# A state-space branch: GpSimd in program order, squares behind the exponentials, last gates on VectorE, one transfer per broadcast decay

## The chip, the cores and the metric

The kernel runs on one core of one Trainium2 chip. The metric is the device time of one execution in microseconds (us). The engines are TensorE (PE in the profile; PEld is its weight load), VectorE (DVE), ScalarE (ACT), GpSimd (POOL) and SyncE (SP, which here only issues DMAs).

## The reference, cut to what matters

One layer of a diffusion backbone over 512 latent tokens and 256 context tokens, model width 1024, all in fp32. One input projection feeds an attention branch and a state-space (SSD) branch; both are merged by gates, projected, and followed by a convolutional feed-forward layer. The change lies in the SSD branch alone: 32 heads of 64 channels in 4 groups of 8, a state of 128, chunks of 128 tokens (4 of the latent tokens, 2 of the context), once forward and once backward.

```python
def ssd_scan(xs, la, bm, cm, h0, with_output):
    ...
    cs = jnp.cumsum(ac, axis=-1)
    decay_to_end = jnp.exp(cs[..., -1:] - cs)
    states = jnp.einsum('bcsgn,bgrcs,bcsgrp->bcgrpn', bc, decay_to_end, xc)
    ...
    states = jnp.einsum('bgrzc,bcgrpn->bzgrpn', chunk_decay, states)
    ...
    cb = jnp.einsum('bclgn,bcsgn->bgcls', cc, bc)
    scores = cb[:, :, None] * jnp.exp(segsum(ac))
    y_diag = jnp.einsum('bgrcls,bcsgrp->bclgrp', scores, xc)
    y_off = jnp.einsum('bclgn,bcgrpn,bgrcl->bclgrp', cc, states[:, :-1], jnp.exp(cs))
    return (y_diag + y_off).reshape(Bsz, L, G, R, P).astype(xs.dtype), final

def ssd_output(y, xs, z, d_skip, g):
    y = y + d_skip.reshape(SSD_GROUPS, SSD_HPG, 1).astype(y.dtype) * xs
    return rmsnorm(y.reshape(Bsz, L, D_SSD) * jax.nn.silu(z), g)
```

## The kernel before

**Weights and products.** An fp32 product is computed as three products of rounded parts. A weight tile of 128x1024 is loaded into `wraw` (three buffers; SP issues the load, L177), ScalarE rounds it into `whi` (L183), VectorE takes the rest into `wlo` (L184), each with two buffers, and TensorE uses them in L238, L239 and L241. Weights of the modulation (`wm`) go into the same three `wraw` buffers but are read by VectorE alone, which sums them into `tm` (L811, L813). So the rounding of a weight, the `wm` sums and all else on VectorE stand in one queue.

**Where the branch lies.** The SSD branch runs from about 430 to 728 us of the span, as 4 groups: group 0 to about 500 us, group 1 to 584, group 2 to 664, group 3 to 728. A list of steps, written by hand, weaves a group's steps with the projections of the next group, whose convolution is the `ta` and `tb` steps L1418 to L1429 on ScalarE and VectorE. Small pieces are put between the products of a projection: `gemm` takes one from the list `BETWEEN` at every third of its blocks.

**A group.** `states` sums the context's states (L1606) from weighted inputs `xw` (VectorE, L1575), and steps the backward states from chunk 3 to chunk 1: a product L1587, the old state times a decay on GpSimd (`st`, L1589), and their sum on VectorE (L1590). Then each of the four chunks has two steps:

- `chunk_in` loads the logarithms of the decays, broadcast to all partitions, into `fb` (L1665, 128x8x128 from `cs_d`, one per direction), and the decays for the earlier states into `far` (L1676, from `us_d`, two DMAs of 64 partitions per direction, three buffers). A product gives C times B, whose diagonal VectorE takes as `cbd` (L1686). From it GpSimd makes `coef` (L1690, L1691) and the diagonal blocks `dg` (L1697, two per chunk, not in chunk 0). ScalarE adds to the logarithms (L1707, L1710) and takes the exponential into `E` (L1714); VectorE merges both directions (the mask, L1711) and multiplies by C times B (L1718); GpSimd adds `dg` (L1720).
- `chunk_out` multiplies the states by C (L1738), VectorE weighs these by `far` into `te` (L1740), TensorE forms the chunk's own part from `E` (L1746), GpSimd adds the two `te` into `y` (L1752), and the forward state moves on (L1587 to L1590 again). A piece `late`, put between later products, adds the parts (VectorE, L1761) and multiplies by the gate `zs` (GpSimd, L1763).

At a group's end `gate` stores the 4 gated tiles to `yz_d` (L1774), and `gates_in` loads the next group's gates into `zs` (L1644, two buffers of four tiles). Squares of the gated tiles for the norm follow one group later, on ScalarE into `sq` (L1566, one buffer), and GpSimd sums them into `ssq` (L1567).

**What sets the order.** Each engine carries out its instructions in order. A scheduler chooses that order at build time by readiness in its own model, except that an instruction given to `keep_in_program_order` stays where the program's text has it. SP's DMAs stand in SP's one queue.

Of the kernel before, what the change touches and what calls it, by code (L numbers as in the profile page):

```python
# [9 lines left out]
F32 = mybir.dt.float32  # L10
# [8 lines left out]
P = 128  # L19
# [25 lines left out]
def tile_hybrid_layer(  # L45
# [219 lines left out]
    ao_d = dpool.tile([8, P, L], F32, name="ao_d")  # L265
    yz_d = dpool.tile([16, P, L], F32, name="yz_d")
    cs_d = dpool.tile([64, L], F32, name="cs_d")
    us_d = dpool.tile([64, L], F32, name="us_d")
    dt_d = dpool.tile([64, L + LC], F32, name="dt_d")
    tt_d = dpool.tile([64, 4], F32, name="tt_d")  # L270
    x1_d = dpool.tile([L, D], F32, name="x1_d")
# [156 lines left out]
    with tc.tile_pool(name="spool", bufs=1) as sp:  # L428
# [177 lines left out]
        def square(x_, q, n, k, x):  # L606
            sq = B_[x, k] = tmp(("ta", "tb")[k % 2])[:, :n] if k else q
            S.activation(sq, x_[:, k, :], AF.Square)
# [605 lines left out]
    def tables():  # L1214
# [6 lines left out]
        def rows(a, x):  # L1221
            return 64 * a + 32 * x, 64 * a + 32 * x + 32
# [51 lines left out]
        def far_out():  # L1274
            for a in range(2):
                for x in range(2):
                    (r0, r1), n = rows(a, x), 128 if x else 384
                    nc.sync.dma_start(us_d[32 * a : 32 * a + 32, 384 * x : 384 * x + n], d["U"][r0:r1, :n])

        def to_end():  # L1280
            cs3, la3 = (d[n].rearrange("p (c t) -> p c t", t=P) for n in ("cs", "la"))
# [152 lines left out]
    def h8(a):  # L1434
        return a.rearrange("p (h d) -> p h d", h=8)

    def bc64(a):
        return a.unsqueeze(2).to_broadcast([P, 8, 64])
# [119 lines left out]
    def square(last=False):  # L1558

        yz = SQUARES.pop(0)  # L1560
        if "ssq" not in F:
            F["ssq"] = True
            tc.keep_in_program_order(S.activation(ssq, yz, AF.Square))
        else:
            sq = tmp("ta") if last else zp.tile([P, 512], F32, tag="th", name="sq", bufs=1)
            tc.keep_in_program_order(S.activation(sq, yz, AF.Square))  # L1566
            G.tensor_tensor(ssq, ssq, sq, ALU.add)  # L1567

    def ssd_steps(g):
        d = GR[g]  # L1570
# [13 lines left out]
        def advance(s, dr, c, xw):  # L1584
            z0 = 32 * dr + 8 * g
            ps = misb()
            T.matmul(ps, d["Bk"][:, c, :], xw, start=True, stop=True)  # L1587
            n = new_state(dr)
            G.tensor_tensor(h8(n), h8(s), bc64(eT[:, z0 : z0 + 8, c]), ALU.mult)  # L1589
            V.tensor_tensor(n, n, ps, ALU.add)  # L1590
            return n

# [61 lines left out]

        def chunk_in(c):

            for _ in range(min(c, 1) + c // 3 if g else 0):
                square()
            fb = []
            for dr in range(2):  # L1660
                f = bp.tile([P, 8, P], F32, tag="fb", name="fb", bufs=4)
                a = bass.AP(
                    tensor=cs_d.tensor, offset=cs_d.offset + (32 * dr + 8 * g) * L + c * P, ap=[[0, P], [L, 8], [1, P]]
                )
                nc.sync.dma_start(f, a)  # L1665
                fb.append(f)
            far = []
            for dr in range(2):
                f = bp.tile([P, 4, P], F32, tag="far", name="far", bufs=FAR)
                for u in range(2):  # L1670
                    a = bass.AP(
                        tensor=us_d.tensor,
                        offset=us_d.offset + (32 * dr + 8 * g + u) * L + c * P,
                        ap=[[0, 64], [2 * L, 4], [1, P]],
                    )
                    nc.sync.dma_start(f[64 * u : 64 * u + 64], a)  # L1676
                far.append(f)
            d["far", c] = far
            d["E"] = []

            def products():
                cb = d["cb"] = misb()
                tok = slice(c * P, (c + 1) * P)
                T.matmul(cb[:, :P], d["BT"][:, tok], d["CT"][:, tok], start=True, stop=True)
                cbd = bp.tile([P, 1], F32, tag="cbd", name="cbd", bufs=2)
                V.tensor_tensor_reduce(  # L1686
                    cb[:, P : 2 * P], cb[:, :P], ident, op0=ALU.mult, op1=ALU.add, scale=1.0, scalar=0.0, accum_out=cbd
                )
                coef = d["coef"] = bp.tile([P, 8], F32, tag="coef", name="coef", bufs=2)
                G.tensor_scalar(coef, TT[:, c, 8 * g : 8 * g + 8], cbd, None, ALU.mult)  # L1690
                G.tensor_tensor(coef, coef, bcs[:, 8 * g : 8 * g + 8], ALU.add)  # L1691
                d["dg"] = [diagonal(q) for q in range(2)] if c else None

            def diagonal(q):
                dg = bp.tile([P, 4, P], F32, tag="dg", name="dg", bufs=2)
                w = d["coef"][:, 4 * q : 4 * q + 4].unsqueeze(2).to_broadcast([P, 4, P])
                G.tensor_tensor(dg, ident.unsqueeze(1).to_broadcast([P, 4, P]), w, ALU.mult)  # L1697
                return dg

            def decays():  # L1700
                for q in range(2):
                    E = bp.tile([P, 4, P], F32, tag="E", name="E", bufs=3)
                    eb = misb()
                    F4 = fb[0][:, 4 * q : 4 * q + 4, :]
                    for u in range(4):
                        h = 8 * g + 4 * q + u
                        e0 = S.activation(E[:, u, :], F4[:, u, :], AF.Identity, bias=TX[:, c, 0, h : h + 1])  # L1707
                        if u == 0 and c:
                            tc.keep_in_program_order(e0)
                        S.activation(eb[:, u * P : (u + 1) * P], fb[1][:, 4 * q + u, :], AF.Identity, bias=TX[:, c, 1, h : h + 1])  # L1710
                    V.copy_predicated(E, sel.unsqueeze(1).to_broadcast([P, 4, P]), eb.rearrange("p (h l) -> p h l", h=4))  # L1711
                    d["E"].append(E)
                for E in d["E"]:
                    S.activation(flat(E), flat(E), AF.Exp)  # L1714

            def weighed():
                for q, E in enumerate(d["E"]):
                    V.tensor_tensor(E, E, d["cb"][:, :P].unsqueeze(1).to_broadcast([P, 4, P]), ALU.mult)  # L1718
                    if c:
                        G.tensor_tensor(E, E, d["dg"][q], ALU.add)  # L1720

            if g in BY_BLOCKS and not c:
                decays()
                BETWEEN[1:2] = [lambda f=BETWEEN[1]: (f(), products(), weighed())]
            else:
                products()
                decays()
                weighed()

        def chunk_out(c):  # L1730
            xs, E, far = d["xs"], d["E"], d.pop(("far", c))
            tok = slice(c * P, (c + 1) * P)
            parts = []
            for dr, s in ((0, d["Sf"]), (1, d["Sb"][c])):
                ps = misb()
                for ct in range(4):
                    z = slice(ct * P, (ct + 1) * P)
                    T.matmul(ps[:, z], s[:, z], d["CT"][:, tok], start=True, stop=True)  # L1738
                t = tmp("te")
                V.tensor_tensor(t, ps, flat(far[dr]), ALU.mult)  # L1740
                parts.append(t)

            yd = misb()
            for h in range(8):
                o = yd[64 * (h % 2) : 64 * (h % 2) + 64, (h // 2) * P : (h // 2 + 1) * P]
                T.matmul(o, xs[:, c, h * 64 : (h + 1) * 64], E[h // 4][:, h % 4, :], start=h < 2, stop=c > 0 and h > 5)  # L1746
            dx = None
            if not c:
                dx = bp.tile([P, 512], F32, tag="dx", name="dx", bufs=1)
                G.tensor_tensor(h8(dx), h8(xs[:, c, :]), bc64(d["coef"]), ALU.mult)  # L1750
            y = bp.tile([P, 512], F32, tag="tf", name="y", bufs=1)
            G.tensor_tensor(y, parts[0], parts[1], ALU.add)  # L1752
            if c < 3:
                d["Sf"] = advance(d["Sf"], 0, c, weigh_in(0, c))

            def late():

                for ct in range(0 if c else 4):
                    z = slice(ct * P, (ct + 1) * P)
                    tc.keep_in_program_order(T.matmul(yd[:, z], dx[:, z], ident, start=False, stop=ct == 3, is_transpose=True))  # L1760
                V.tensor_tensor(y, yd, y, ALU.add)  # L1761
                z = d["zt"][:, :, tok]
                G.tensor_tensor(z, y.rearrange("p (a t) -> p a t", a=4), z, ALU.mult)  # L1763

            assert not BETWEEN
            if g < 3:
                BETWEEN.extend([lambda: None] * 4 + [lambda: (late(), turn(1)), turn])
            else:
                BETWEEN.extend([lambda: None] * 2 + [late])
# [650 lines left out]
```

## Time and profile before

| | |
|---|---|
| median of 3 runs | 1233.85 us (1233.82 to 1236.01) |
| the profiled execution, its own time | 1233.18 us |
| its span in the profile | 1231.4 us |
| TensorE busy | 1209.4 us, 98% |
| VectorE, ScalarE, GpSimd busy | 932.3, 682.3, 266.7 us |
| mean granted clock of TensorE | 0.995 |

The profile gives, for each engine, when each instruction began, how long it took and, in brackets, how long the engine had stood idle before it and what released it. The waits are summed per line: "PE mis L1746 <- POOL E L1720: 10.0, 7, 3.7" is 10.0 us in 7 waits, the longest 3.7. A table of stretches gives the busy time of PE, PEld, DVE, ACT and POOL, then the granted clock of TensorE as a fraction, the busy share of the 16 DMA engines, and GB/s. For DMAs a row gives the count, KB each, and the median us from issue to landing. Names are those of the code, without buffer numbers.

### The profile page before, as it was taken

Reading aid. Unit: us, or ns where it says so; the run is one execution under the profiler, and the core shown is the slowest. Engines: PE = TensorE matmul, PEld = TensorE weight load, DVE = VectorE, ACT = ScalarE, POOL = GpSimd, SP = SyncE. Lnnn points to the kernel's source line nnn. Section 1 sums busy time; section 2 is a strip of 40 time slices with the busy share of each in tenths; the row PEclk is TensorE's granted clock in tenths of the full one; section 3 lists DMA queues with packets and bytes.
Section 4 is the critical chain, followed back from the end, with each engine's and each line's share of the span. In section 5 each row is a group of like instructions: output and inputs, shape, how many; then the busy total and the mean of one; then the engine's idle time right before and its main releaser. Section 6 shows DMA issues by size and latency. Waiting matters only on the chain.

```text
span 1231.4 us, 17909 instructions
## 1 busy us (share of the span) xinstructions
PE 1209.4 (98%) x6429; PEld 1009.0 (82%) x6429; DVE 932.3 (76%) x1494; ACT 682.3 (55%) x1267; POOL 266.7 (22%) x278
## 2 busy tenths in 40 slices
PE   9999999999999999999998989999999999999998
PEld 6798888888888888778876868888988888888886
DVE  5857787888565697787885966777688777778787
ACT  5658788787544376465564645223544434436654
POOL 0000121101003555373571752000200110010021
PEclk9999999999999999999999989999999999999999
DMA  9645799744759447347467657677356633436752
GB/s 369 253 136 182 158 248 258 170 153 126 179 168 265 144 131 226 118 134 224 130 167 225 180 185 268 223 252 238 85 126 161 207 112 128 144 96 217 221 185 97
DMA packets 142025, 224.30 MB, mean 182 GB/s; under 512 B 27784, under 2 KB 87344, under 8 KB 141936
## 3 DMA queue, kind: packets, MB, share of 16 engines
q1 hardware_dynamic: 127856, 195.61, 50.8%
q0 software_dynamic: 13792, 27.27, 9.9%
q8 instruction: 51, 0.84, 0.3%
q14 instruction: 38, 0.31, 0.1%
q10 hardware_dynamic: 288, 0.27, 0.1%
HBM read 196.17 MB, written 45.02 MB: 196 GB/s over the span
## 4 chain that ended last, share of the span: by engine, by line
PE 81%; DVE 7%; issue 3%; DMA 3%; POOL 3%; ACT 2%; SPq 0%; DVEq 0%; ACTq 0%; POOLq 0%
PE acc L238 17%; PE acc L239 17%; PE acc L241 17%; PE score L979 3%; PE po L1028 3%; PE pt L1015 2%; PE mis L582 2%; PE mis L2278 2%; PE mis L2276 2%; PE mis L2277 2%; DMA wraw<-wm 1%; PE acc L2278 1%; PE acc L2276 1%; PE acc L2277 1%; PE acc L1098 1%
## 5 line engine op out<-in xcount | busy, mean ns | idle before, releaser
L183 ACT CAST whi<-wraw 128x1024 fp32r<-128x1024 f32 (+1 forms) x115 | 120.1, 1045 | 151.8 <-PE acc L239 109.5
L184 DVE TENSOR_TENSOR wlo<-wraw,whi 128x1024 fp32r<-128x1024 f32 (+1 forms) x115 | 146.6, 1275 | 67.5 <-ACT whi L183 65.2
L238 PE MATMUL acc<-hlh,whi 128*128 128x512 f32 x472 | 195.1, 413 | 0.0
L239 PE MATMUL acc<-hll,whi 128*128 128x512 f32 x472 | 186.2, 395 | 0.0
L241 PE MATMUL acc<-hlh,wlo 128*128 128x512 f32 x472 | 185.9, 394 | 0.0
L238 PE MATMUL acc<-mh,whi 128*128 128x512 f32 x368 | 143.4, 390 | 0.0
L241 PE MATMUL acc<-mh,wlo 128*128 128x512 f32 x368 | 143.4, 390 | 0.0
L239 PE MATMUL acc<-ml,whi 128*128 128x512 f32 x368 | 143.3, 390 | 0.0
L241 PEld LDWEIGHTS acc<-hlh,wlo 128*128 128x128 f32 x472 | 89.4, 189 | 19.6
L238 PEld LDWEIGHTS acc<-hlh,whi 128*128 128x128 f32 x472 | 89.7, 190 | 18.4 <-issue 3.2
L239 PEld LDWEIGHTS acc<-hll,whi 128*128 128x128 f32 x472 | 89.7, 190 | 17.6 <-issue 2.4
L238 PEld LDWEIGHTS acc<-mh,whi 128*128 128x128 f32 x368 | 69.1, 188 | 14.4
L239 PEld LDWEIGHTS acc<-ml,whi 128*128 128x128 f32 x368 | 69.1, 188 | 14.3
L241 PEld LDWEIGHTS acc<-mh,wlo 128*128 128x128 f32 x368 | 69.1, 188 | 14.2
L164 POOL DMA_DIRECT2D dsum<-wdn x24 | 25.2, 1118 | 194.9 <-DVE wlo L1112 184.0
L988 DVE CUSTOM_DVE_ANT_0 p<-score,winm,nsink 128x512 f32<-128x512 f32 (+1 forms) x64 | 51.8, 810 | 15.4 <-PE score L979 13.9
L813 DVE SCALAR_TENSOR_TENSOR tm<-wraw,csil,tm 128x512 f32<-128x512 f32 x56 | 46.3, 827 | 17.1 <-DMA wraw<-wm 16.4
L995 ACT ACTIVATE p<-p,mneg 128x512 f32<-128x512 f32 (+1 forms) x64 | 49.7, 778 | 15.4 <-DVE mneg L988 14.8
L1418 ACT ACTIVATE ta<-acc,half 128x512 f32<-128x512 f32 (+1 forms) x66 | 46.6, 707 | 17.0 <-PE acc L241 15.7
L1023 DVE TENSOR_TENSOR ptl<-pt,pth 128x512 fp32r<-128x512 f32 x72 | 47.5, 685 | 8.8 <-ACT pth L1019 7.7
L238 PE MATMUL acc<-hch,whi 128*128 128x256 f32 x176 | 53.2, 302 | 0.0
L1419 DVE SCALAR_TENSOR_TENSOR ta<-acc,half,ta 128x511 f32<-128x511 f32 (+1 forms) x66 | 43.7, 662 | 12.6 <-ACT ta L1418 12.5
(453 smaller groups left out, 3069.6 us busy)
## 6 DMA issues: line engine op xcount, KB each, us to landing
wraw<-wup SPq DMA_DIRECT2D x44, 512.0 KB, 3.9
dsum<-wdn POOLq DMA_DIRECT2D x24, 704.0 KB, 8.6
wraw<-wm SPq DMA_DIRECT2D x32, 512.0 KB, 4.2
fb<-cs_d SPq DMA_DIRECT2D x32, 512.0 KB, 6.8
wraw<-wx SPq DMA_DIRECT2D x24, 512.0 KB, 4.2
wm<-wm SPq DMA_DIRECT2D x16, 512.0 KB, 8.0
wraw<-wz SPq DMA_DIRECT2D x16, 512.0 KB, 4.1
far<-us_d SPq DMA_DIRECT2D x64, 128.0 KB, 4.0
```

The source lines that it names most:

```text
L183: F["cast"] = S.copy(hi[:, :n], r[:, :n])
L184: F["sub"] = V.tensor_tensor(lo[:, :n], r[:, :n], raw(hi[:, :n]), ALU.subtract)
L238: T.matmul(ps, wh, xh[:, k0 + k, :], start=a, stop=False)
L239: T.matmul(ps, wh, xl[:, k0 + k, :], start=False, stop=False)
L241: T.matmul(ps, wl, xh[:, k0 + k, :], start=False, stop=b)
L813: V.scalar_tensor_tensor(acc, r[:, u * 512 : u * 512 + 512], sc, acc, ALU.mult, ALU.add)
L988: V.tensor_tensor_reduce(p[:, :w], d["ps"][i][:, o0 : o0 + w], m, op0=ALU.add, op1=ALU.min, scale=1.0, scalar=nsink[:, h : h + 1], accum_o ...
L995: S.activation(p, p, AF.Exp, bias=d["mneg"][:, i : i + 1], scale=-1.0, accum_out=d["den"][:, i : i + 1])
L1023: V.tensor_tensor(d["ptl"][x], d["pt"][x], raw(d["pth"][x]), ALU.subtract)
L1418: S.activation(o[:, :n], ps[:, :n], AF.Identity, scale=hcol(base_w, stride + i), bias=hcol(base_b, i))
L1419: x = V.scalar_tensor_tensor(o[:, 1:n], ps[:, 0 : n - 1], hcol(base_w, i), o[:, 1:n], ALU.mult, ALU.add)
L2276: T.matmul(ps, h, wh, start=st, stop=False, skip_group_check=True)
```

## The change

Five things are changed.

1. GpSimd's operations of the branch (`st`, `coef`, `dg`, `E`, `dx`, `y`, the gate, `ssq`) keep the order of the program's text.
2. A square no longer stands at the start of `chunk_in` but behind its exponentials, one each in chunks 1, 2 and 3, and a fourth behind chunk 3's gate.
3. In `chunk_out` the forward state's step stands ahead of `y`.
4. The gate of chunk 3 (four of sixteen) is multiplied on VectorE.
5. `us_d` is laid out anew, so that one DMA of 128 partitions and 256 KB brings what two of 64 partitions and 128 KB brought: 32 loads of `far` for 64. It is written by 8 stores of 128 columns for 4 of up to 384.

```diff
-    us_d = dpool.tile([64, L], F32, name="us_d")
+    us_d = dpool.tile([4, 2, 2, 4, 4, P], F32, name="us_d")
...
         def far_out():
             for a in range(2):
                 for x in range(2):
-                    (r0, r1), n = rows(a, x), 128 if x else 384
-                    nc.sync.dma_start(us_d[32 * a : 32 * a + 32, 384 * x : 384 * x + n], d["U"][r0:r1, :n])
+                    r0, r1 = rows(a, x)
+                    for c in range(1 if x else 3):
+                        o = us_d[3 * x + c, :, a].rearrange("u g j t -> (g j) u t")
+                        nc.sync.dma_start(o, d["U"][r0:r1, c * P : c * P + P])
...
             tc.keep_in_program_order(S.activation(sq, yz, AF.Square))
-            G.tensor_tensor(ssq, ssq, sq, ALU.add)
+            tc.keep_in_program_order(G.tensor_tensor(ssq, ssq, sq, ALU.add))
+
+    def gp(*a):
+        return tc.keep_in_program_order(G.tensor_tensor(*a))
+
+    def gs(*a):
+        return tc.keep_in_program_order(G.tensor_scalar(*a))
...
-            G.tensor_tensor(h8(n), h8(s), bc64(eT[:, z0 : z0 + 8, c]), ALU.mult)
+            gp(h8(n), h8(s), bc64(eT[:, z0 : z0 + 8, c]), ALU.mult)
...
         def chunk_in(c):
 
-            for _ in range(min(c, 1) + c // 3 if g else 0):
-                square()
...
-                for u in range(2):
-                    a = bass.AP(
-                        tensor=us_d.tensor,
-                        offset=us_d.offset + (32 * dr + 8 * g + u) * L + c * P,
-                        ap=[[0, 64], [2 * L, 4], [1, P]],
-                    )
-                    nc.sync.dma_start(f[64 * u : 64 * u + 64], a)
+                a = bass.AP(
+                    tensor=us_d.tensor,
+                    offset=us_d[c, 0, dr, g].offset,
+                    ap=[[32 * P, 2], [0, 64], [1, 512]],
+                )
+                nc.sync.dma_start(flat(f), a)
...
                     if c:
-                        G.tensor_tensor(E, E, d["dg"][q], ALU.add)
+                        gp(E, E, d["dg"][q], ALU.add)
...
                 products()
                 decays()
                 weighed()
+            if g and c:
+                square()
...
-                G.tensor_tensor(h8(dx), h8(xs[:, c, :]), bc64(d["coef"]), ALU.mult)
-            y = bp.tile([P, 512], F32, tag="tf", name="y", bufs=1)
-            G.tensor_tensor(y, parts[0], parts[1], ALU.add)
+                gp(h8(dx), h8(xs[:, c, :]), bc64(d["coef"]), ALU.mult)
             if c < 3:
                 d["Sf"] = advance(d["Sf"], 0, c, weigh_in(0, c))
+            y = bp.tile([P, 512], F32, tag="tf", name="y", bufs=1)
+            gp(y, parts[0], parts[1], ALU.add)
...
-                G.tensor_tensor(z, y.rearrange("p (a t) -> p a t", a=4), z, ALU.mult)
+                x = y.rearrange("p (a t) -> p a t", a=4)
+                if c == 3:
+                    V.tensor_tensor(z, x, z, ALU.mult)
+                else:
+                    gp(z, x, z, ALU.mult)
+                if g and c == 3:
+                    square()
```

GpSimd's row around chunk 2 of group 1, before the change: from the sum `y` of chunk 1 to `y` of chunk 2 (each row is a line of the code, the operation, what it writes and reads, and its shape).

```order
L1752 TENSOR_TENSOR y<-te 128x512
L1567 TENSOR_TENSOR ssq<-ssq,sq 128x512
L1589 TENSOR_TENSOR st<-st,eT 128x512
L1690 TENSOR_SCALAR coef<-TT,cbd 128x8
L1691 TENSOR_TENSOR coef<-coef,bcs 128x8
L1697 TENSOR_TENSOR dg<-ident,coef 128x512 x2
L1763 TENSOR_TENSOR zs<-y,zs 128x4x128
L1567 TENSOR_TENSOR ssq<-ssq,sq 128x512
L1720 TENSOR_TENSOR E<-E,dg 128x512 x2
L1567 TENSOR_TENSOR ssq<-ssq,sq 128x512
L1752 TENSOR_TENSOR y<-te 128x512
```

The same stretch of GpSimd's row after the change; lines 1569, 1572 and 1575 are those of `ssq` and of the two helpers.

```order
L1572 TENSOR_TENSOR st<-st,eT 128x512
L1572 TENSOR_TENSOR y<-te 128x512
L1575 TENSOR_SCALAR coef<-TT,cbd 128x8
L1572 TENSOR_TENSOR coef<-coef,bcs 128x8
L1572 TENSOR_TENSOR dg<-ident,coef 128x512 x2
L1572 TENSOR_TENSOR E<-E,dg 128x512 x2
L1569 TENSOR_TENSOR ssq<-ssq,sq 128x512
L1572 TENSOR_TENSOR zs<-y,zs 128x4x128
L1572 TENSOR_TENSOR st<-st,eT 128x512
L1572 TENSOR_TENSOR y<-te 128x512
```

`E` now stands directly behind `dg`; `ssq` and the gate `zs` have moved behind `E`. The `st` of the third row before is the forward state's step to the end of chunk 2; after the change that is the `st` of the last but one row, behind `E`, `ssq` and `zs` (the `st` of the first row is chunk 1's).

SP's queue from chunk 2 of group 2 to the end of that group, before the change (an `x4` is four DMAs in a row):

```order
L1676 DMA far<-us_d 64x4x128 x4
L177 DMA wraw<-wm 128x1024
L1644 DMA zs<-zs_d 128x512 x4
L1665 DMA fb<-cs_d 128x8x128
L177 DMA wraw<-wg 128x1024
L1665 DMA fb<-cs_d 128x8x128
L177 DMA wraw<-wg 128x1024
L1676 DMA far<-us_d 64x4x128 x4
L1774 DMA yz_d<-zs 128x512 x4
L1665 DMA fb<-cs_d 128x8x128
L1816 DMA ta<-yz_d 128x512 x2
L177 DMA wraw<-wm 128x1024
```

The same stretch after the change:

```order
L177 DMA wraw<-wm 128x1024
L1681 DMA far<-us_d 128x1x512 x2
L1671 DMA fb<-cs_d 128x8x128 x2
L177 DMA wraw<-wg 128x1024 x2
L1681 DMA far<-us_d 128x1x512
L1652 DMA zs<-zs_d 128x512 x3
L1787 DMA yz_d<-zs 128x512 x4
L1652 DMA zs<-zs_d 128x512
L1681 DMA far<-us_d 128x1x512
L1671 DMA fb<-cs_d 128x8x128
L1829 DMA ta<-yz_d 128x512
L177 DMA wraw<-wm 128x1024
```

`wm` has moved ahead of a chunk's `far`; the four `zs` loads have moved behind the next group's first `far`, three ahead of the `yz_d` stores and one behind them; each four `far` are two, now of 128 partitions.

More of the change, by code (lines that the diff above doesn't have):

```diff
@@ L1689, in products @@
                 coef = d["coef"] = bp.tile([P, 8], F32, tag="coef", name="coef", bufs=2)
-                G.tensor_scalar(coef, TT[:, c, 8 * g : 8 * g + 8], cbd, None, ALU.mult)
-                G.tensor_tensor(coef, coef, bcs[:, 8 * g : 8 * g + 8], ALU.add)
+                gs(coef, TT[:, c, 8 * g : 8 * g + 8], cbd, None, ALU.mult)
+                gp(coef, coef, bcs[:, 8 * g : 8 * g + 8], ALU.add)
                 d["dg"] = [diagonal(q) for q in range(2)] if c else None
@@ L1696, in diagonal @@
                 w = d["coef"][:, 4 * q : 4 * q + 4].unsqueeze(2).to_broadcast([P, 4, P])
-                G.tensor_tensor(dg, ident.unsqueeze(1).to_broadcast([P, 4, P]), w, ALU.mult)
+                gp(dg, ident.unsqueeze(1).to_broadcast([P, 4, P]), w, ALU.mult)
                 return dg
```

## The prediction

> **What bounds the kernel now.** I read the page first, then the waits of the tensor engine, then the time line of each engine around the longest of them.
>
> ```profile
> span 1231.4 us, 17909 instructions
> PE 1209.4 (98%) x6429; PEld 1009.0 (82%) x6429; DVE 932.3 (76%) x1494; ACT 682.3 (55%) x1267; POOL 266.7 (22%) x278
> ...
> PE mis L1746 <- POOL E L1720: 10.0, 7, 3.7
> PE mis L1606 <- DVE xw L1575: 3.2, 1, 3.2
> ```
>
> TensorE is the bound: 98% busy, 22.0 us not. Of these, 10.0 us are one wait: the products L1746 stand for `E`, whose last step is GpSimd's sum L1720. Another 3.2 us is a wait for `xw`. Here are these waits in TensorE's time line (start, length, wait in brackets), then VectorE and SP around the second kind:
>
> ```profile
> 544.66 1.95 PE L1738 MATMUL mis<-CT,st 128*128 128x128 f32 x16
> 549.61 1.09 PE L1746 MATMUL mis<-E,xs 128*64 128x128 f32 x16 [2.99 <-POOL E L1720]
> ...
> 631.12 0.66 PE L1746 MATMUL mis<-E,xs 128*64 128x128 f32 x8 [1.00 <-POOL E L1720]
> 632.35 0.66 PE L1746 MATMUL mis<-E,xs 128*64 128x128 f32 x8 [0.58 <-POOL E L1720]
> ...
> 646.99 0.66 PE L1746 MATMUL mis<-E,xs 128*64 128x128 f32 x8 [1.02 <-POOL E L1720]
> ...
> 724.33 0.81 PE L1746 MATMUL mis<-E,xs 128*64 128x128 f32 x8 [3.72 <-POOL E L1720]
> 725.55 1.12 PE L1746 MATMUL mis<-E,xs 128*64 128x128 f32 x8 [0.41 <-POOL E L1720]
> ...
> 660.53 0.48 SPq L177 DMA_DIRECT2D wraw<-wm  x1
> 668.11 1.54 DVE L813 SCALAR_TENSOR_TENSOR tm<-wraw,csil,tm 128x512 f32<-128x512 f32 x2 [5.10 <-DMA wraw<-wm]
> ```
>
> So four places wait for `E`: group 1 chunk 2, group 2 chunks 2 and 3, group 3 chunk 3. After the first and last the clock drops as well (columns: PE, PEld, DVE, ACT, POOL busy, then PEclk, DMA share, GB/s):
>
> ```profile
> 540.00:560.00 20.00, 16.95 (x107) 14.16 (x106) 15.39 (x28) 15.13 (x40) 15.11 (x17) 0.91 0.48 126
> 720.00:740.00 20.00, 15.86 (x71) 12.44 (x70) 12.36 (x16) 9.35 (x15) 8.53 (x6) 0.83 0.55 184
> ```
>
> 0.09 x 20 = 1.8 us and 0.17 x 20 = 3.4 us go there. All that the change could win is then 10.0 + 1.8 + 3.4 + 3.2 = 18.4 us.
>
> **The new order on GpSimd and ScalarE.** Chunk 2 of group 1, GpSimd's rows and VectorE's two that feed them:
>
> ```profile
> 540.96 1.06 POOL L1589 TENSOR_TENSOR st<-st,eT 128x512 f32<-128x512 f32 x1 [0.95 <-DVE st L1590]
> 541.02 0.13 DVE L1686 DVE_READ_ACCUMULATOR2_ANT cbd<- 128x1 f32 x1
> 542.00 0.30 POOL L1690 TENSOR_SCALAR coef<-TT,cbd 128x8 f32<-128x8 f32 x1
> 542.67 2.04 POOL L1697 TENSOR_TENSOR dg<-ident,coef 128x512 f32<-128x512 f32 x2
> 544.67 1.27 POOL L1763 TENSOR_TENSOR zs<-y,zs 128x512 f32<-128x512 f32 x1
> 545.90 1.26 POOL L1567 TENSOR_TENSOR ssq<-ssq,sq 128x512 f32<-128x512 f32 x1
> 547.12 2.49 POOL L1720 TENSOR_TENSOR E<-E,dg 128x512 f32<-128x512 f32 x2
> ...
> 544.09 0.69 DVE L1718 TENSOR_TENSOR E<-E,mis 128x512 f32<-128x512 f32 x1 [0.35 <-ACT E L1714]
> ```
>
> VectorE's `E` was done at 544.78 and `dg` at 544.71, but the sum began at 547.12: `zs` and `ssq`, 2.5 us, stood ahead of it. Now both stand behind. TensorE is ready at 544.66 + 1.95 = 546.6; the sum would run from 544.8 to 547.3, or earlier, since the state's step `st` (1.06 us) no longer stands ahead of `coef`, which then waits only for `cbd` (541.15). ScalarE gains too, since a square no longer stands between the exponentials:
>
> ```profile
> ACT sq L1566 <- POOL ssq L1567: 10.4, 3, 5.5
> ```
>
> These 10.4 us, in which ScalarE stood for a buffer that GpSimd's `ssq` sum held, go; there is one square per chunk, and its predecessor's sum is long done. I take stalls one to three as gone: 2.99 + 1.8 + 1.58 + 1.3 (1.02, and 0.3 that the 10.0 us hold beyond the rows above) = 7.7 us. In group 3 chunk 3 VectorE itself is late:
>
> ```profile
> 720.22 1.30 DVE L1718 TENSOR_TENSOR E<-E,mis 128x512 f32<-128x512 f32 x2
> 720.80 1.27 POOL L1763 TENSOR_TENSOR zs<-y,zs 128x512 f32<-128x512 f32 x1
> 722.02 3.48 POOL L1720 TENSOR_TENSOR E<-E,dg 128x512 f32<-128x512 f32 x2
> ```
>
> Only `zs` (1.2 us) can be passed; 720.9 is then the start, and TensorE was ready at 720.5. I take 1.4 us here and leave the clock's 3.4 as unknown. The order is worth 9.1 us, say 9; its ends are 18.4 (everything goes) and 4 (only the 2.5 us of `zs` and `ssq` in the first stall, and 1.5 us in the three later places together).
>
> What could be late next: `st` stands behind `E`, `ssq` and `zs` now, and VectorE's sum L1590 waits for it. GpSimd needs 1.3 + 1.3 + 1.1 = 3.7 us for the three after `E`; L1590 comes behind 1.1 us of L1746, behind the product L1587, and on VectorE behind two `te`, a `tc` and often a `wlo`. I cost it at nothing, and at up to 2 us a chunk if that cover fails, which the range of the order's gain takes in.
>
> **The last gates on VectorE.** Four times one tensor product, by the nearest row 0.68 us on VectorE, against 1.27 us on GpSimd above:
>
> ```profile
> L1740 DVE TENSOR_TENSOR te<-mis,far x32: 673/676/683, 442.3 to 723.7; 128x512 f32<-128x512 f32 x32
> ```
>
> VectorE is 76% busy, and behind the gate stand the `ta` steps that drain accumulators. 4 x 0.68 = 2.7 us, taken at nothing, since the store behind it starts as much earlier; ends 0 and 2.7.
>
> **The gate loads on SP.** A group's four `zs` loads stood early in the group; three now stand behind its first `far`, and the fourth behind the `yz` stores. A group's last square is later now, and its buffer is what they wait for. They move 1 MB into the stretch where `yz`, `fb` and `wm` queue. Against it, `wm` goes ahead of `far` in chunk 3 of groups 1 and 2. Nothing for both, ends -2 and +3 us.
>
> **One transfer per decay.**
>
> ```profile
> 535.37 2.57 SPq L1676 DMA_DIRECT2D far<-us_d  x4
> ...
> 352.39 1.70 SPq L1278 DMA_DIRECT2D us_d<-dU  x4
> ```
>
> Of 64 `far` loads 32 stay, with twice the bytes each: 32 issues of 0.6 us less on SP, which waits for buffers anyway: nothing. Four more `us_d` stores of 0.4 us, with a weight load behind them: nothing, at most 2 us. What matters is how such a load is spread. Before, its source has 64 equal rows outermost and its target 64 partitions. Now the source is written as 2 blocks, each repeated 64 times. No row of before has a transfer with so few entries outermost, so the trace does not show on how many of the 16 DMA engines it runs. One end: all 16; it is then cheaper than now. The other end: the spread follows the outermost step, and a transfer runs on 2 engines. I take two, because an even cut along the outermost step is what the 64 rows of before allowed and the 2 blocks do not.
>
> The Trainium skill, page "DMA: Bandwidth & Descriptors", section "Rules for kernel authors", says that an outermost dimension smaller than 16 confines a DMA to as many engines at most, and names a leading broadcast; by it this is two engines, and the sum is the one below. No run shows it yet.
>
> The price on two engines:
>
> ```profile
> wraw<-wm SPq DMA_DIRECT2D x32, 512.0 KB, 4.2
> fb<-cs_d SPq DMA_DIRECT2D x32, 512.0 KB, 6.8
> ...
> far<-us_d SPq DMA_DIRECT2D x64, 128.0 KB, 4.0
> ...
> 0.00:60.00 60.00, 58.14 (x391) 42.68 (x392) 40.67 (x89) 32.93 (x62) 2.51 (x11) 1.00 0.81 310
> ...
> 500.00:584.00 84.00, 80.54 (x483) 66.10 (x482) 66.68 (x99) 50.39 (x118) 42.58 (x38) 0.98 0.56 156
> 584.00:664.00 80.00, 77.15 (x475) 64.11 (x474) 65.21 (x95) 50.03 (x118) 44.69 (x39) 1.00 0.59 165
> 664.00:728.00 64.00, 56.69 (x308) 43.76 (x307) 47.35 (x67) 34.86 (x83) 42.46 (x39) 0.97 0.59 186
> ```
>
> A busy DMA engine moved 310 / (0.81 x 16) = 23.9 GB/s in the stretch of large rows. Half of 2 x 128 KB is 131 KB, 5.5 us on each of the two; a group's eight loads are 44 us. Those two also carry a sixteenth of the rest. In group 1 that is 0.56 x 84 = 47 us less the `far` of now (2.1 of 13.1 MB, 7.5 us), 39.5; with 44 it is 83.5 of 84 us: full. Group 2: 47.2 - 7.5 + 44 = 83.7 of 80, 4 us too much. Group 3: 37.8 - 6.7 + 44 = 75 of 64, 11 too much. That makes 15 us from the amount alone, which is the lower end. On top comes the queue: what is issued behind one or two `far` ends 5.5 or 11 us later. `wm` is what hurts, since VectorE takes it in order, with `wlo` and `xw` behind (the 5.1 us wait above, and TensorE's 3.2 us behind that). In front of each of groups 1 to 3 one `wm` stands so; one `far` each makes 16.5 us, two make 33. I take 15 + 16 = 31, ends 15 and 48.
>
> **The sum.** 1231.4 - 9 + 31 = 1253.4 us of span. The profiled execution took 1233.18, 1.8 over its span, so 1255.2; the median of the runs, 1233.85, lies 0.7 above that execution: 1256.
>
> **Rivals.**
> 1. All 16 engines carry the new load; the order's gain stands alone. For it: every transfer of before runs so, as far as landing times tell (4.0 us for `far`, 64 partitions). Against: none of them has a small outermost step. 1233.85 less 9, and some 3 more, as the decays need fewer pieces and `xw`'s wait shrinks: 1222, between 1215 and 1230. This one is faster, and decides as soon as a `far` lands in about 5 us, as before, with 256 KB.
> 2. Two engines, but the rest hides it. For it: weights and `far` are loaded well ahead, here by 10.9 us (issue, then the cast that reads it) and by 18 (the `far` of 535.37 above, then `te`). Against: `wm`, which is not.
>
> ```profile
> 564.19 0.33 SPq L177 DMA_DIRECT2D wraw<-wx  x1
> 575.08 1.04 ACT L183 CAST whi<-wraw 128x1024 fp32r<-128x1024 f32 x1
> ...
> 553.69 0.68 DVE L1740 TENSOR_TENSOR te<-mis,far 128x512 f32<-128x512 f32 x1
> ```
>
> Then only the amount costs, its lower end of 15, against a gain of 9 to 18: 1231 to 1240, say 1235, no change that could be told.
> 3. The order doesn't do what it says: `E` stays late since VectorE's masks are, as in group 3. Against: 544.78 against 547.12 above. It only takes 5 us off the gain, and is in the ranges.
>
> **How the numbers follow.** Two engines and slower 0.56 (1240 to 1280, likeliest 1256); rival 2 0.10; rival 1 0.34. 2.5 us, 0.2%, is about what can be told from no change. Faster: 0.33 of rival 1 and 0.01 of rival 2, 0.34. Same: 0.01 of rival 1 and 0.06 of rival 2, 0.07. Slower: the rest, 0.59. The range must reach over both signs: from 1220 (two thirds of rival 1) to 1277 (most of the likeliest) it holds 0.8.
>
> **What the profile will show.** Right on the order: no L1746 wait for GpSimd in groups 1 and 2, GpSimd's `E` directly behind `dg`, no `sq` wait for `ssq`. Right on the load: `far` lands in 8 us or more, `wraw` and `fb` in well over their 4.2 and 6.8 us, and new waits of VectorE for `wm` and of ScalarE for `fb`, with TensorE behind them, most in group 3. Wrong: `far` lands in 4 to 6 us; then rival 1 holds. It would also be wrong, the other way, if the two engines fall so far behind that whole chunks wait for `far` itself, over 1280.

## The result, and the profile after

| | before | changed |
|---|---|---|
| median | 1234.59 us (1233.82 to 1236.01, 4 runs) | 1267.14 us (1266.48 to 1268.07, 4 runs) |
| ratio to before | | 1.0263, interval 1.0245 to 1.0281 |
| span of the profiled execution | 1231.4 us | 1265.3 us |
| mean granted clock | 0.995 | 0.983 |

The change is slower by 32.5 us. The forecast was slower, 1256 us, with a range of 1220 to 1277.

The page of the changed kernel, its span and TensorE's row:

```profile
span 1265.3 us, 17888 instructions
PE 1219.7 (96%) x6429; PEld 1014.3 (80%) x6429; DVE 933.3 (74%) x1498; ACT 681.6 (54%) x1267; POOL 259.5 (21%) x274
```

The span grew by 33.9 us. TensorE stood for 45.6 us where it had stood for 22.0, which is 23.6; and the same 6429 products took 1219.7 us for 1209.4, 10.3 us more, at a granted clock of 0.983 for 0.995. The waits, summed per line (us in total, times, longest):

```profile
DVE tm L813 <- DMA wraw<-wm: 48.7, 12, 12.9
ACT E L1712 <- DMA fb<-cs_d: 28.1, 6, 13.7
...
PE mis L1614 <- DVE xw L1583: 9.2, 1, 9.2
PE mis L1595 <- DVE xw L1583: 6.5, 2, 4.9
PE acc L238 <- DVE ta L1424: 6.3, 1, 6.3
PE mis L1753 <- POOL E L1572: 5.6, 8, 1.2
```

VectorE waits for `wm` three times as long as before (16.4 us there), ScalarE for `fb`, for which it hardly waited (3.3 us), and TensorE behind both: `wm` and `fb` take 3% each of the chain that ended last. The old wait for `E` (now L1753) is 5.6 us for 10.0, and none is over 1.2; ScalarE's wait of `sq` for `ssq` is 3.1 us, one wait, for 10.4.

What the new loads do shows where little else moves. This is a stretch in which two `far` are on their way, issued from 450.67 on, with no other load of SP behind them until 455.89 (columns: length, then busy time and count of PE, PEld, DVE, ACT, POOL; then PEclk, DMA share, GB/s):

```profile
453.50:455.80 2.30, 2.30 (x11) 1.88 (x10) 1.72 (x3) 2.30 (x10) 2.12 (x3) 1.00 0.13 52
```

0.13 of 16 engines is two engines, and they move 52 GB/s, 26 each. A load of 256 KB is then 5.0 us on them; the prediction had 5.5.

Now the first place where TensorE stands, ahead of group 0: SP's queue, then the chain of waits from there on (start, length, what).

```profile
370.46 3.66 SPq L1681 DMA_DIRECT2D far<-us_d  x2
374.17 7.64 SPq L1652 DMA_DIRECT2D zs<-zs_d  x4
381.86 0.55 SPq L1671 DMA_DIRECT2D fb<-cs_d  x1
382.51 7.15 SPq L177 DMA_DIRECT2D wraw<-wm  x1
```

```profile
382.51 13.28 DMA wraw<-wm
395.81 0.75 DVE tm L813
396.56 0.60 DVE CT L1431
397.17 0.66 DVE tm L813
397.83 0.67 DVE ta L1421
398.52 0.76 DVE ta L1424
399.42 0.55 PE acc L238
```

Two `far`, four `zs` and an `fb` stand ahead of `wm`. SP needs 7.15 us to issue this one `wm`, and it has landed after 13.3. VectorE takes it in order, with the convolution's `ta` behind, and TensorE starts its next product at 399.42 after 6.35 us of waiting.

### The profile page after: what moved, and what is told of

It reads as the page before. It is cut to its first block, busy times and chain, and to the rows that moved or that the text cites. A ratio compares the mean times of both kernels' runs of the same rounds, so it can differ in the third digit from the quotient of the medians.

```text
span 1265.3 us, 17888 instructions
## 1 busy us (share of the span) xinstructions
PE 1219.7 (96%) x6429; PEld 1014.3 (80%) x6429; DVE 933.3 (74%) x1498; ACT 681.6 (54%) x1267; POOL 259.5 (21%) x274
## 4 chain that ended last, share of the span: by engine, by line
PE 75%; DMA 9%; DVE 8%; ACT 4%; issue 3%; POOL 1%; SPq 0%; DVEq 0%; ACTq 0%; POOLq 0%
PE acc L238 15%; PE acc L239 15%; PE acc L241 15%; DMA wraw<-wm 3%; DMA fb<-cs_d 3%; PE score L979 3%; PE po L1028 3%; PE pt L1015 2%; PE mis L582 2%; PE mis L2291 2%; PE mis L2290 2%; PE mis L2289 2%; PE acc L2291 1%; PE acc L2290 1%; PE acc L2289 1%
## 5 line engine op out<-in xcount | busy, mean ns | idle before, releaser
L813 DVE SCALAR_TENSOR_TENSOR tm<-wraw,csil,tm 128x512 f32<-128x512 f32 x56 | 43.7, 780 | 49.5 <-DMA wraw<-wm 48.7
L1712 ACT ACTIVATE E<-fb,TX 128x128 f32<-128x128 f32 x128 | 45.0, 389 | 31.2 <-DMA fb<-cs_d 28.1
L1430 ACT ACTIVATE tb<-ta 128x512 f32<-128x512 f32 (+1 forms) x44 | 23.4, 532 | 56.9 <-DVE ta L1424 56.8
```

The source lines that it names most:

```text
L813: V.scalar_tensor_tensor(acc, r[:, u * 512 : u * 512 + 512], sc, acc, ALU.mult, ALU.add)
```

## The experiments

All twelve were timed against the kernel before on the same chip; the ratio is what is compared.

**On how many engines the load runs.** Five runs change only the form of the `far` loads. With four blocks the order of the branch on SP, VectorE, ScalarE and GpSimd is that of the changed kernel; in the other four some rows of the queues moved along with it.

*Two halves*: the new layout of `us_d`, but two loads per tile.

```diff
+                for u in range(2):
-                    ap=[[32 * P, 2], [0, 64], [1, 512]],
+                    ap=[[0, 64], [1, 512]],
-                nc.sync.dma_start(flat(f), a)
+                nc.sync.dma_start(flat(f)[64 * u : 64 * u + 64], a)
```

> The changed kernel, but each far tile comes by two loads of 64 partitions again (64 equal rows of 2 KB outermost in the source, new layout of us_d kept). Spread theory (the load runs on as many DMA engines as its outermost step has entries, and that is the whole loss): 1222 us, between 1215 and 1230; wraw<-wm lands in about 4 us, and no wait of VectorE for wm over 5 us. Order theory (the new order or the later gate loads lose the time, the load is harmless): 1262 to 1270, as the changed kernel. Layout theory (the 2 KB rows of the new layout are slow to read however they are spread): over 1245.

*Four, eight and sixteen blocks*: `us_d` holds each block 2, 4 or 8 times (a store with a repeated source), and one load per tile reads 4, 8 or 16 blocks.

```diff
-    us_d = dpool.tile([4, 2, 2, 4, 4, P], F32, name="us_d")
+    us_d = dpool.tile([4, 2, 2, 2, 4, 4, P], F32, name="us_d")
...
-                    ap=[[32 * P, 2], [0, 64], [1, 512]],
+                    ap=[[32 * P, 4], [0, 32], [1, 512]],
```

> The changed kernel, but us_d holds each block twice, so that the source of a far load is written as 4 blocks, each repeated 32 times; bytes, rows and number of loads as in the changed kernel, and the order on all engines too. Spread theory: four engines, a load takes 2.8 us on each instead of 5.5, a group's eight 22 us on top of some 40 of 84: no engine is overfull, two far delay what is behind them by 5.5 instead of 11 us: 1235 us, between 1226 and 1245. Theories that blame the order, or the size of 256 KB in one transfer: 1262 to 1270.

> As the run with four blocks, but 8 blocks, each repeated 16 times. Spread theory: eight engines, 1.4 us on each per load: 1224 us, between 1218 and 1232. Order or size theory: 1262 to 1270.

> The changed kernel with us_d holding each block 8 times, so that a far load's source is 16 blocks, each repeated 8 times: one transfer of 128 partitions still. Spread theory: as the run with two halves, 1227 us, between 1224 and 1231. If one transfer for two saves anything of its own: 1221 to 1224. If what the run with eight blocks had left over (6 us above two halves) is the size of the transfer or the copies, not the spread: 1231 to 1234.

*One of two*: the forward `far` as changed, the backward one in two halves.

> The changed kernel, but only the forward direction's far comes in one load of two blocks; the backward one comes in two halves. Two engines then carry 22 us per group beside some 40 of 84 and are not overfull, but a load still takes 5.5 us on each. If the loss is the amount (an overfull pair of engines falls behind): 1230 to 1238 us. If each such load costs the same, whatever the amount: half the way, 1244 to 1250.

The loss below is the ratio less that of two halves, times 1234.6; by the intervals it is good to about 3 us. The third column is an estimate of what a group's eight `far` put on the busiest engine, by the 23.9 GB/s of the prediction.

| run | median | us on the busiest engine, per group | ratio to before | loss |
|---|---|---|---|---|
| changed, 2 blocks | 1267.14 | 44 | 1.0263 (1.0245 to 1.0281) | 39.6 |
| four blocks | 1236.04 | 22 | 1.0017 (1.0003 to 1.0031) | 9.3 |
| one of two | 1234.60 | 25 | 1.0003 (0.9988 to 1.0018) | 7.5 |
| eight blocks | 1232.88 | 11 | 0.9987 (0.9973 to 1.0000) | 5.6 |
| sixteen blocks | 1227.37 | 5.5 | 0.9940 (0.9927 to 0.9954) | -0.2 |
| two halves | 1227.05 | 5.5 | 0.9942 (0.9920 to 0.9964) | 0 |

With 16 blocks the very same transfer of 256 KB costs nothing, and with fewer the loss rises with what stands on the busiest engine: 22 and 25 us cost the same, within the intervals, whether four engines carry all loads or two carry half of them, and 44 us cost four to five times as much. So it is neither the size of the transfer, nor the layout, nor the order. One transfer for two also saves nothing by itself. Two expectations were narrowly missed: eight blocks lie above their 1218 to 1232, and with two halves VectorE's longest wait for `wm` was 5.6 us, not under 5 (5.1 before). With four and eight blocks SP still stood for up to 5.0 and 4.8 us over one `wm`, with sixteen for 0.4.

The spread itself shows where two `far` of the same chunk are under way, with four blocks and with eight (columns as above):

```profile
447.00:449.00 2.00, 2.00 (x10) 1.68 (x9) 1.24 (x2) 2.00 (x8) 1.84 (x3) 1.00 0.26 102
```

```profile
447.40:448.40 1.00, 1.00 (x6) 0.83 (x5) 1.00 (x2) 1.00 (x5) 0.87 (x2) 1.00 0.52 201
```

That is four engines of 16 and eight, at 25 GB/s each. By the rule of the Trainium skill, page "DMA: Bandwidth & Descriptors", section "Rules for kernel authors", an outermost dimension smaller than 16 confines a DMA to as many engines at most; the traces agree (0.13, 0.26 and 0.52 of 16 with two, four and eight blocks), and so does the loss by the load on the busiest engine.

*The load alone*, put into the kernel before:

> The kernel before with the one-transfer loads alone (new layout, stores and loads; order, squares and gates as before). Spread theory: slower by what the changed kernel lost plus the order's gain, 1234.6 + 32.5 + 9 = 1276 us, between 1268 and 1285. Order theory: 1230 to 1236. If the changed kernel's later gate loads or earlier wm are part of the loss, in between: 1245 to 1265.

Measured 1274.70 us, ratio 1.0330 (1.0303 to 1.0358), 40.7 us slower; the same two waits are there:

```profile
DVE tm L813 <- DMA wraw<-wm: 48.0, 14, 13.2
ACT E L1708 <- DMA fb<-cs_d: 24.0, 3, 14.0
```

So the load costs 40 us with the old order and with the new.

*The loads from ScalarE's queue*: `nc.scalar.dma_start` for `nc.sync.dma_start`, nothing else.

> The changed kernel, but the far loads (two blocks outermost, as changed) are issued from ScalarE's queue, so that SP never stands in front of a full queue. If the loss is mostly that SP stands still and nothing behind it starts on any engine: 1228 to 1245 us, unless ScalarE stands in its turn. If it is mostly that two engines have too much to move and every other transfer ends with its share on them: 1250 to 1270.

Measured 1287.45 us, ratio 1.0437 (1.0417 to 1.0456): slower still, above both expectations. The lengths of one DMA issue (ns, least/median/most) of `fb` before, of `fb` in the changed kernel, and of `far` in this run, then ScalarE and SP in this run:

```profile
L1665 SPq DMA_DIRECT2D fb<-cs_d x32: 360/441/969, 363.5 to 690.7; - x32
```

```profile
L1671 SPq DMA_DIRECT2D fb<-cs_d x32: 370/591/6245, 362.7 to 722.2; - x32
```

```profile
L1681 ACTq DMA_DIRECT2D far<-us_d x32: 489/490/7673, 365.7 to 770.2; - x32
```

```profile
366.81 8.21 ACTq L1681 DMA_DIRECT2D far<-us_d  x2
375.07 2.16 ACT L1712 ACTIVATE E<-fb,TX 128x128 f32<-128x128 f32 x7 [8.15 <-issue]
```

```profile
370.27 15.75 SPq L1652 DMA_DIRECT2D zs<-zs_d  x4
```

An issue of `fb` that took at most 1.0 us before takes up to 6.2 in the changed kernel, and in this run a `far` holds ScalarE for up to 7.7 us. Behind it stands whatever else that engine has to do: ScalarE stood 8.15 us ahead of its activation at 375.07. SP did not become free by this: its four `zs`, issued while ScalarE issued the two `far`, took 15.75 us, for 7.64 in the changed kernel. So the run does not divide the loss between this standing and the overfull engines, since SP stood on and ScalarE stood too; that division stays open.

**What the order is worth.** *All of the change but the loads*:

> All of the change but the loads: program order on GpSimd, squares behind the exponentials, the state ahead of y, last gates on VectorE; far and us_d as in the kernel before. If the order is worth what the prediction said and the layout of two 64-partition loads is neutral: as the run with two halves, 1227 us, between 1224 and 1230. If a part of that run's gain came from the new layout (2 KB rows): 1229 to 1233.

*Program order on GpSimd alone*, and *the squares' place alone*:

> The kernel before with program order for GpSimd's operations alone (squares, y, gates and loads as before). If the gain comes from E standing directly behind dg: 1226 to 1229 us, and ScalarE's wait of sq for ssq stays. If the squares' place is what matters (the wait of ScalarE for the sq buffer, 10.4 us before): 1232 to 1236.

> The kernel before with the squares behind the exponentials alone. If the squares' place is what matters: 1226 to 1229 us. If program order is: 1231 to 1236, with waits of L1746 for E that stay at 5 us or more.

*The order, but the last gates on GpSimd*:

> As the run of the order alone, but chunk 3's gates stay on GpSimd. The prediction put the move at nothing: 1226 us, within 1.5 of the order alone. If the 2 us by which the whole order beats the sum of its two tried parts (2.5 and 3.8 of 8.2) come from these gates: 1228.

| run | median | ratio to before |
|---|---|---|
| order alone | 1226.08 | 0.9931 (0.9918 to 0.9943) |
| program order alone | 1231.69 | 0.9977 (0.9966 to 0.9987) |
| squares alone | 1230.46 | 0.9964 (0.9952 to 0.9976) |
| order, gates on GpSimd | 1226.88 | 0.9937 (0.9924 to 0.9949) |

The order is worth 8.2 us by the medians, and the layout nothing that can be told. Each of the two parts measured between its two expectations, so neither alone is the one that matters: program order brought 2.5 us and left ScalarE's wait of `sq` for `ssq` (8.3 us) and 8.0 us of TensorE's waits for `E`, the squares brought 3.8 us and left 6.2 us of waits for `E`. Together they leave 1.5 us, so in these waits the two do more than their sum. In the medians the whole gains 1.8 us more than the two, which the intervals do not tell from nothing; `st` ahead of `y` was not tried apart. The gates make no difference that can be told. Here is chunk 2 of group 1 in the run of the order alone, GpSimd and then TensorE, as shown of before in the prediction, and that run's waits of TensorE:

```profile
539.84 2.04 POOL L1570 TENSOR_TENSOR dg<-ident,coef 128x512 f32<-128x512 f32 x2
541.84 2.54 POOL L1570 TENSOR_TENSOR E<-E,dg 128x512 f32<-128x512 f32 x2
544.34 1.27 POOL L1567 TENSOR_TENSOR ssq<-ssq,sq 128x512 f32<-128x512 f32 x1
545.57 1.28 POOL L1570 TENSOR_TENSOR zs<-y,zs 128x512 f32<-128x512 f32 x1
...
546.20 1.09 PE L1752 MATMUL mis<-E,xs 128*64 128x128 f32 x16
```

```profile
PE mis L1612 <- DVE xw L1581: 3.3, 1, 3.3
PE mis L1449 <- DVE tc L1429: 2.7, 4, 1.0
PE mis L1752 <- POOL E L1570: 1.5, 3, 1.0
```

`E` follows `dg` at once and is done at 544.4, where it had been done at 549.6; TensorE takes it at 546.2 without a wait, where it had waited 2.99 us.

**A version that beats both.** The largest wait left, `xw`, stands behind a `wm` that SP issues behind `yz`, `zs` and `fb`. *wm ahead* is the order alone, with one step of the written list moved in group 3:

```diff
-        prog += s[0:1] + f + b[0:1] + s[1:2] + s[10:11] + m[0:1] + b[1:2]
+        prog += s[0:1] + f + b[0:1] + s[1:2] + (b[1:2] + s[10:11] + m[0:1] if g == 3 else s[10:11] + m[0:1] + b[1:2])
```

> As the run of the order alone, but in group 3 the second weight of the modulation and its sum stand one step later in the list, behind the next projection's first weight, so that SP issues it ahead of fb and yz. If TensorE's wait for xw behind it (3.3 us in the order alone) goes: 1223 us, between 1221 and 1225. If another wait takes its place: 1226 or more.

Measured 1222.12 us, ratio 0.9899 (0.9884 to 0.9915). The wait for `xw` fell to 1.2 us:

```profile
PE mis L1612 <- DVE xw L1581: 1.2, 1, 1.2
```

That is 2.1 us of the 3.7 by which the span is shorter (1220.6 for 1224.3). The rest is in TensorE's products, which took 1205.6 us for 1207.2.

## Why the prediction was right, and where it was off

**The order: 9 us forecast, 8.2 measured.** The stalls went as its rows said, and `E` of chunk 2 was done earlier still than the 547.3 of its working, since VectorE's `E` came earlier too (done at 542.8 for 544.8). VectorE's `te` of group 1's last chunk began 4.4 us earlier than before, against the 4.8 us (2.99 and 1.8) of the first stall. That the sums agree is partly luck: TensorE's waits for `E` fell by 8.5 us (10.0 to 1.5) where the prediction counted 7.3, since in group 3 it gave back 1.4 of 4.1 us and only 1.0 was left; against that, VectorE's `tc` became late (2.7 us in 4 waits, 0.4 before), and not the `st` that it had named.

**Gates at nothing**: 0.9931 and 0.9937, the same. The `zs` loads and `wm`, taken at nothing, were measured only as part of the order alone, which agrees with it.

**Two engines**: right, and so was the sign.

**The load's price: 31 us forecast, 40 measured.** This is the term that was mis-sized, and its division was wrong as well. It had two parts: 15 us because groups 2 and 3 would carry more than the two engines can in their length, and 16 us for one `wm` in front of each of groups 1 to 3. The first `te` of each group in the changed kernel, and below it in the run of two halves:

```profile
449.97 0.68 DVE L1747 TENSOR_TENSOR te<-mis,far 128x512 f32<-128x512 f32 x1
...
536.64 0.68 DVE L1747 TENSOR_TENSOR te<-mis,far 128x512 f32<-128x512 f32 x1
...
625.80 0.68 DVE L1747 TENSOR_TENSOR te<-mis,far 128x512 f32<-128x512 f32 x1
...
716.42 1.27 DVE L1747 TENSOR_TENSOR te<-mis,far 128x512 f32<-128x512 f32 x2
```

```profile
441.77 0.68 DVE L1748 TENSOR_TENSOR te<-mis,far 128x512 f32<-128x512 f32 x1
...
519.58 0.68 DVE L1748 TENSOR_TENSOR te<-mis,far 128x512 f32<-128x512 f32 x1
...
600.31 0.68 DVE L1748 TENSOR_TENSOR te<-mis,far 128x512 f32<-128x512 f32 x1
...
684.89 1.28 DVE L1748 TENSOR_TENSOR te<-mis,far 128x512 f32<-128x512 f32 x2
```

The lag is 8.2, 17.1, 25.5 and 31.5 us, so it grows by 8.2, 8.9, 8.4 and 6.0 per group and by some 8 more to the end. In groups 0 to 2 it does not grow from the first chunk to the third; it comes ahead of group 0 and at the ends of groups, where `far`, `zs`, `fb` and `wm` stand together. In group 3 it grows by 8.5 us between the second chunk and the third, where SP issued a weight `wg` behind two `far` and ScalarE waited for it:

```profile
748.42 1.05 ACT L183 CAST whi<-wraw 128x1024 fp32r<-128x1024 f32 x1 [10.93 <-DMA wraw<-wg]
```

So the sum over a group's length said little: the price is paid in bursts, where a load that is needed soon stands behind `far`. In the prediction's own terms, the places in front of groups 1 to 3, put at 16 us, cost 23 (8.9, 8.4 and 6.0); the place ahead of group 0, which it left out, cost 8; and against the 15 us from the amount, 4 in group 2 and 11 in group 3, stand only the last 8, all in group 3. So two terms were too small, by 7 and by 8, and one too large by 7, and the 9 us by which the price was missed are what is left of that. The prediction saw the mechanism, `wm` behind `far`, but took weights as loaded well ahead and did not see that SP itself would stand. "Most in group 3" was wrong too: the longest waits for `wm` and for `fb`, 12.9 and 13.7 us, stand ahead of group 0.

**The signs in the profile.** The waits of VectorE for `wm` and of ScalarE for `fb`, with TensorE behind them, came as named. The page of the changed kernel gives no landing times for SP's loads, so "8 us or more" is not shown; the chain gives 13.3 us for one `wm`. The waits for `E` in groups 1 and 2 went where the load is harmless (0.5 us left there in the order alone, and 1.0 in group 3), and not fully beside it (5.6 in all). ScalarE's wait of `sq` for `ssq`, which was to go, kept 3.1 us, at the last square of group 3.

**The rivals.** "All 16 engines" is what the runs of sixteen blocks and of two halves show: 1227, inside the 1215 to 1230 given for it. "Hidden by the rest" was wrong for two engines (39.6 us), and nearly right for four (9.3, against a gain of 8). The third, `E` late behind VectorE's masks, is refuted by the order alone, where `E` was early.

## What to carry to other kernels

Before two transfers are merged into one, look at what stands outermost in both its patterns: a broadcast written as "2 blocks, each repeated 64 times" ran on two DMA engines at 52 GB/s, and the 40 us that this cost hid a gain of 8 from the same change; the same 256 KB with 16 blocks outermost cost nothing. Price a slow transfer not by the average load of the stage, but at the places where urgent loads are queued behind it. And split a change of several parts when its sum is bad: its order alone, with one load moved ahead, gave 1222 us.

## What was not expected of the hardware

A DMA issue is not free of what is under way: one `wm` held SP for 7.1 us (before at most 0.5) and one `far` held ScalarE for 7.7 us when loads of two engines were ahead, and SP stood behind loads that ScalarE had issued. And a stall cost more than its length, since the granted clock was lower behind it. The 30 us behind the first stall, in the changed kernel and in the run of two halves:

```profile
400.00:430.00 30.00, 30.00 (x162) 26.47 (x162) 21.21 (x35) 13.76 (x22) 19.17 (x30) 0.94 0.59 176
```

```profile
400.00:430.00 30.00, 30.00 (x161) 24.80 (x160) 20.77 (x33) 10.78 (x18) 15.50 (x23) 1.00 0.48 145
```

TensorE is busy for all 30 us in both, and by the clock 0.06 x 30 = 1.8 us are lost in the one. All of it lies in the first 6 us; from 406 on the clock is 1.00 again:

```profile
399.00:402.00 3.00, 2.58 (x12) 2.61 (x13) 2.24 (x5) 2.02 (x3) 0.00 (x0) 0.50 0.45 123
402.00:406.00 4.00, 4.00 (x22) 3.70 (x22) 3.39 (x6) 1.53 (x3) 3.79 (x7) 0.80 0.89 244
406.00:410.00 4.00, 4.00 (x20) 3.34 (x20) 3.75 (x7) 2.13 (x5) 1.50 (x3) 1.00 0.42 133
```

Over the whole kernel 23.6 us more of standing went with 10.3 us more of slower products.
